# Four pairs of split weights, loads of summed blocks earlier in the program, and two dealing rates for the side pieces

## The chip, the core and the metric

The kernel runs on one core of one Trainium2 chip. The metric is device time in microseconds (us). PE is TensorE, the engine of the matmuls (PEld its weight loads), DVE is VectorE, ACT is ScalarE, POOL is GpSimd, and SP is the queue that issues nearly all loads.

## The reference

Three transformer-like layers on a batch of one, 256 tokens of 2048 channels, in float32: a layer with gated linear attention beside dilated attention, then a gated feed-forward of 5632 channels, then a retention and convolution layer, then a windowed attention layer. The part that matters here is the feed-forward:

```python
h2 = rms_norm(x, norm2_g[l])
x = x + (jax.nn.silu(h2 @ w_gate[l]) * (h2 @ w_up[l])) @ w_down[l]
```

`w_gate` and `w_up` are 2048 by 5632, `w_down` is 5632 by 2048. All weights are read once, 384 MB in float32.

## The kernel before

**Split products.** Each matrix product is made of three matmuls in a fast float32 form. Both operands are split into a high part (`hi`, rounded) and a low part (`lo`, what is left): `three` (line 184) issues xh·hi, xh·lo and xl·hi. A weight tile is 128 partitions by 2 by 512 (512 KB). `split` (line 158) makes one pair from it: a cast on ACT writes `hi` (line 160), a subtraction on DVE writes `lo` (line 161). The pairs live in the pool `hl_p`, which holds three of them: the cast of the fourth pair waits until PE has used the first.

**Streams.** `linear` (line 189) loads weight tiles into `raw` buffers (five of them), splits them, and multiplies each with both halves of the tokens: 12 matmuls of 512 columns for a tile. After each 3 matmuls it calls `deal` (line 178), which takes a piece from the deque `side` at every `pace[0]`-th call and writes it into the program at that point.

**The feed-forward stage.** The 5632 hidden channels are 11 blocks of 512. `plain(0)` computes block 0 directly. Then five passes follow (the loop over `w`, line 696): `seven(2w+1)` puts 28 side pieces into the deque; `plain(2w+2)` computes the next block as a stream (64 calls of `deal`); `down` multiplies two finished blocks with `w_down` (another 64 calls); `drain` empties what is left. The side pieces compute their block for gate and up with seven products instead of eight, in the manner of Strassen and Winograd: a product uses a half of the tokens alone, so a tile is worth 6 matmuls.

- Twelve pieces (`first`, line 634) load a tile into a `raw` buffer and split it, as a stream does.
- Sixteen pieces (`rest`, line 652; four steps `kp` of four pieces `n`) need sums of weight blocks. For each `kp` four blocks b12, b11, b22, b21 are loaded into a ring of six tiles (`block_tile`, line 610; the tags b0, b1, nh, nl, u10, u11, which show as `b` and `u` in a trace). Each piece then makes one DVE subtraction of 128 by 1024 (line 665, called a sum from here), splits its result and multiplies. The sums of a step are: n=0 needs b11 and b12, n=1 needs b12 and b22, n=2 needs b22 and b11, n=3 needs b22 and b21.

A tile of the ring is free for a new load once the last reader of its previous block is done: b22 of one step takes the tile of b12 of the step before, which the `lo` of that step's piece n=1 releases; b11 of one step takes the tile of b21 two steps before, and so on.

**What sets the order.** The program is written in the order just told, but a scheduler places the instructions of each engine by its own estimate of when their inputs are there. Each engine then runs its list in order: on DVE a sum that waits for a load holds up every `lo` behind it, and on SP a load that waits for its tile holds up every load behind it.

Of the kernel before, what the change touches and what calls it, by code (L numbers as in the profile page):

```python
# [25 lines left out]

CU, CR, CIND, CID, CMASK, COMASK, CGE, CLE, CGT, COROPE, CEND = 0, 128, 256, 258, 386, 514, 642, 770, 898, 1026, 1282


def _constants():  # L30
# [7 lines left out]
    c[:, CMASK:CMASK + P] = same & (s <= t)  # L38
    c[:, COMASK:COMASK + P] = np.where(s >= t, 0.0, NEG)
    c[:, CGE:CGE + P] = s >= t  # L40
    c[:, CLE:CLE + P] = s <= t
    c[:, CGT:CGT + P] = s > t

# [7 lines left out]
    co, so = angles(64)  # L51
    c[:, COROPE:COROPE + 128] = np.concatenate([co, co], 2).reshape(P, 128)
    c[:, COROPE + 128:COROPE + 256] = np.concatenate([-so, so], 2).reshape(P, 128)

# [24 lines left out]
def model(ctx, tc, a, out):  # L79
    nc = tc.nc  # L80
    cst = ctx.enter_context(tc.tile_pool(name="cst", bufs=1))
    raw_p = ctx.enter_context(tc.tile_pool(name="raw_p", bufs=5))
    hl_p = ctx.enter_context(tc.tile_pool(name="hl_p", bufs=3))
    xt_p = ctx.enter_context(tc.tile_pool(name="xt_p", bufs=4))
# [245 lines left out]
    for c0, n in ((2688, 400), (2304, 384), (2048, 256)):  # L330
        accs = linear(w_in, c0, n, full(st), got, fine=n == 400)
        got = []
        if n == 400:
            for b in range(4):
                got.append(fetch(w_in, b, 2304, 384))
                if b == 2:
                    tc.keep_in_program_order(nc.sync.dma_start(cm, a["c_main"]))
                cs = slice(b * 512, (b + 1) * 512)
# [7 lines left out]
            tc.keep_in_program_order(nc.gpsimd.dma_start(rb[0:32, :], a["rel_bias"]))  # L346
            sink = cst.tile([P, 32], F32, tag="sink", name="sink")
            tc.keep_in_program_order(nc.gpsimd.dma_start(sink, a["od_sinks_2"].partition_broadcast(P)))
            qkw = cst.tile([P, 2, 64], F32, tag="qkw", name="qkw")
            tc.keep_in_program_order(nc.gpsimd.dma_start(qkw[:, 0, :], a["od_q_norm_w_2"].partition_broadcast(P)))  # L350
            tc.keep_in_program_order(nc.gpsimd.dma_start(qkw[:, 1, :], a["od_k_norm_w_2"].partition_broadcast(P)))
            V.tensor_scalar(gc[:, NQ:NQ + 1], gc[:, NQ:NQ + 1], float(P) ** -0.5, None, ALU.mult)
# [277 lines left out]
    def seven(j):  # L630
# [4 lines left out]
        def first(kp, n):  # L635
# [14 lines left out]
            silu_gate(sg[:, 0], c11, rh[:, 0:1])  # L650

        def rest(kp, n):
            if n == 0:
                b12, b11, b22, b21 = [block_tile() for _ in range(4)]
                rows(b12, w_up, 2 * kp, c0)
                rows(b11, w_gate, 2 * kp, c0)
                rows(b22, w_up, 8 + 2 * kp, c0)
                rows(b21, w_gate, 8 + 2 * kp, c0)
                c["b"] = (b11, b12, b21, b22)
                if kp == 0:  # L660
                    c["P"] = [work_bank() for _ in range(3)] + [ps_acc.tile([P, 512], F32, tag="acc", name=nm("acc"))]
            b11, b12, b21, b22 = c["b"]
            dst, x0, x1, which = ((b11, b12, b11, "S1"), (b12, b22, b12, "S3"), (b22, b22, b11, "S2"),
# [6 lines left out]
        def last():  # L670
# [150 lines left out]

    ra = cst.tile([P, 2, 2, 64], F32, tag="ra", name="ra")
    rbt = cst.tile([P, 2, 2, 64], F32, tag="rbt", name="rbt")
    co = cm[:, COROPE:COROPE + 128].rearrange("p (t d) -> p t d", t=2)
    si = cm[:, COROPE + 128:COROPE + 256].rearrange("p (t d) -> p t d", t=2)
    for w in range(2):
# [52 lines left out]
    def att_scores(c):  # L879
# [47 lines left out]
    def att_turn(c):  # L927
# [5 lines left out]
        for k in range(t + 1):  # L933
# [117 lines left out]
```

## Time and profile before

| | us |
|---|---|
| median of 3 runs | 1947.53 (1945.02 to 1947.83) |
| the profiled execution, its own time | 1947.46 |
| its span on the core | 1945.7 |
| outside the span | 1.8 |

| engine | busy us | share of the span |
|---|---|---|
| PE | 1912.6 | 98% |
| DVE | 1280.0 | 66% |
| ACT | 970.4 | 50% |
| POOL | 193.3 | 10% |

The granted TensorE clock is full (1.00, the 2.4 GHz level) in every slice. PE's busy time is that of matmuls whose records overlap: each is recorded for some 390 ns, while the next starts 227 ns later, so a share of 98% does not say that matmuls start as often as they could. The feed-forward passes lie between about 500 and 1130 us of the span.

### The profile page before, as it was taken

The numbers are of one execution on the slowest core, as the hardware profiler recorded it, in microseconds if no ns is written. First come the engines' busy times: TensorE is split into PE (matmuls) and PEld (weight loads), VectorE is DVE, ScalarE is ACT, GpSimd is POOL, SyncE is SP. The second block draws the span as 40 slices with busy tenths as digits, with TensorE's granted clock in tenths as the row PEclk, the third lists the DMA queues.
The fourth block names the chain that finished last, engine by engine and source line by source line (L and its number), as shares of the span: only waits on it lengthen the run. The fifth ranks groups of instructions, "written<-read, shape, count | busy, mean of one in ns | idle before, by whom it ended". The sixth has DMA issues, their size and how long they took to land.

```text
span 1945.7 us, 23810 instructions
## 1 busy us (share of the span) xinstructions
PE 1912.6 (98%) x8808; PEld 1565.8 (80%) x8808; DVE 1280.0 (66%) x1486; ACT 970.4 (50%) x1313; POOL 193.3 (10%) x314
## 2 busy tenths in 40 slices
PE   8999999999999999999999999999999999999999
PEld 8877888888778778777777788888888888788787
DVE  5445555686787886886877875555555565777654
ACT  6544544455545545445445454444444454566543
POOL 2000221110000000000000001010000003754100
PEclk9999999999999999999999999999999999999999
DMA  8675665567778778777777566666666556544464
GB/s 303 196 213 150 179 174 173 172 203 250 239 218 248 229 224 256 230 228 239 244 226 244 191 175 183 174 182 172 186 193 192 188 183 191 166 138 133 141 200 146
DMA packets 202644, 387.72 MB, mean 199 GB/s; under 512 B 12296, under 2 KB 20512, under 8 KB 202400
## 3 DMA queue, kind: packets, MB, share of 16 engines
q1 hardware_dynamic: 201472, 382.52, 64.6%
q0 software_dynamic: 912, 3.64, 0.7%
q8 instruction: 69, 1.13, 0.2%
q14 instruction: 47, 0.39, 0.1%
q10 hardware_dynamic: 144, 0.05, 0.0%
HBM read 384.04 MB, written 3.68 MB: 199 GB/s over the span
## 4 chain that ended last, share of the span: by engine, by line
PE 82%; DVE 7%; DMA 6%; issue 3%; POOL 1%; ACT 1%; SPq 0%; DVEq 0%; ACTq 0%
PE acc L186 24%; PE acc L187 24%; PE acc L185 24%; DVE lo L161 4%; DMA raw<-in_w_down_dram 3%; DVE b L665 2%; DMA b<-in_w_up_dram 2%; PE at L187 2%; PE at L186 2%; PE at L185 2%; DVE u L665 1%; DMA u<-in_w_up_dram 1%; PE at L950 1%; ACT hi L160 1%; PE tr L223 1%
## 5 line engine op out<-in xcount | busy, mean ns | idle before, releaser
L161 DVE TENSOR_TENSOR lo<-raw,hi 128x1024 fp32r<-128x1024 f32 (+3 forms) x646 | 790.5, 1226 | 491.4 <-ACT hi L160 484.1
L160 ACT CAST hi<-raw 128x1024 fp32r<-128x1024 f32 (+3 forms) x646 | 670.8, 1039 | 696.6 <-PE acc L187 604.2
L186 PE MATMUL acc<-lo,xh 128*128 128x512 f32 (+3 forms) x1640 | 640.5, 391 | 3.4 <-DVE lo L161 3.4
L187 PE MATMUL acc<-hi,xl 128*128 128x512 f32 (+3 forms) x1640 | 634.6, 387 | 0.0
L185 PE MATMUL acc<-hi,xh 128*128 128x512 f32 (+3 forms) x1640 | 592.1, 389 | 5.3 <-ACT hi L160 5.3
L186 PEld LDWEIGHTS acc<-lo,xh 128*128 128x128 f32 x1640 | 308.9, 188 | 66.9 <-DVE lo L161 6.2
L185 PEld LDWEIGHTS acc<-hi,xh 128*128 128x128 f32 x1640 | 307.3, 188 | 68.5 <-ACT hi L160 5.6
L187 PEld LDWEIGHTS acc<-hi,xl 128*128 128x128 f32 x1640 | 309.0, 188 | 60.4 <-issue 2.1
L186 PE MATMUL acc<-lo,mh 128*128 128x512 f32 x640 | 253.9, 398 | 13.8 <-DVE lo L161 13.4
L187 PE MATMUL acc<-hi,ml 128*128 128x512 f32 x640 | 248.8, 391 | 0.0
L185 PE MATMUL acc<-hi,mh 128*128 128x512 f32 x640 | 231.7, 393 | 1.0 <-ACT mh L160 1.0
L186 PEld LDWEIGHTS acc<-lo,mh 128*128 128x128 f32 x640 | 120.1, 188 | 49.9 <-DVE lo L161 26.3
L185 PEld LDWEIGHTS acc<-hi,mh 128*128 128x128 f32 x640 | 119.4, 188 | 26.3 <-ACT mh L160 1.2
L187 PEld LDWEIGHTS acc<-hi,ml 128*128 128x128 f32 x640 | 120.1, 188 | 23.9 <-DVE ml L161 0.2
L160 ACT CAST hi<-b 128x1024 fp32r<-128x1024 f32 x54 | 57.0, 1055 | 90.5 <-PE acc L187 90.5
L161 DVE TENSOR_TENSOR lo<-b,hi 128x1024 fp32r<-128x1024 f32 x54 | 65.8, 1219 | 20.6 <-ACT hi L160 20.6
L709 POOL DMA_DIRECT2D u<-in_c_even_dram x1 | 0.6, 635 | 679.5 <-PE at L187 679.5
L186 PE MATMUL at<-lo,u 128*128 128x512 f32 x160 | 62.9, 393 | 4.1 <-DVE lo L161 4.1
L187 PE MATMUL at<-hi,u 128*128 128x512 f32 x160 | 62.4, 390 | 0.0
L185 PE MATMUL at<-hi,u 128*128 128x512 f32 x160 | 62.3, 389 | 0.0
L252 DVE TENSOR_TENSOR x<-x,acc 128x512 f32<-128x512 f32 x88 | 57.2, 679 | 6.9 <-PE acc L187 6.9
L665 DVE TENSOR_TENSOR b<-b,b 128x1024 f32<-128x1024 f32 x41 | 50.0, 1219 | 11.8 <-DMA b<-in_w_up_dram 11.2
(252 smaller groups left out, 1554.9 us busy)
## 6 DMA issues: line engine op xcount, KB each, us to landing
raw<-in_ev_w_in_dram SPq DMA_DIRECT2D x128, 512.0 KB, 3.8
raw<-in_w_gate_dram SPq DMA_DIRECT2D x88, 512.0 KB, 4.4
raw<-in_w_down_dram SPq DMA_DIRECT2D x88, 512.0 KB, 4.8
raw<-in_w_in_dram SPq DMA_DIRECT2D x80, 512.0 KB, 3.8
raw<-in_od_w_in_dram SPq DMA_DIRECT2D x72, 512.0 KB, 3.6
raw<-in_w_up_dram SPq DMA_DIRECT2D x68, 512.0 KB, 4.6
raw<-in_w_out_dram SPq DMA_DIRECT2D x32, 512.0 KB, 3.6
raw<-in_ev_w_out_dram SPq DMA_DIRECT2D x32, 512.0 KB, 3.7
```

The costliest lines, as they stand in the source:

```text
L160: A.copy(hi, src)
L161: V.tensor_tensor(lo, src, hi.bitcast(F32), ALU.subtract)
L185: T.matmul(o, xh, hi, start=start, stop=False)
L186: T.matmul(o, xh, lo, start=False, stop=False)
L187: T.matmul(o, xl, hi, start=False, stop=stop)
L223: T.transpose(ps[:, k * S + t * P:k * S + (t + 1) * P], x[:, t, c:c + P], ident)
L252: V.tensor_tensor(xs, xs, accs[t], ALU.add)
L665: V.tensor_tensor(dst, x0, x1, ALU.subtract)
L709: nc.gpsimd.dma_start(ce, a["c_even"][:, :512])
L950: T.matmul(pv[e * 64:(e + 1) * 64, :S], vo[:, k, g * 64:(g + 1) * 64], PT[:, :, e], start=k == 0, stop=k == t)
```

## The change

Three edits concern the feed-forward stage:

1. `hl_p` holds four pairs of split weights, not three.
2. The loads of the summed blocks are taken out of `rest` and written by a new function `ahead`, which is called four pieces earlier: those of step 0 in the last four of the twelve first pieces, those of step kp+1 in the pieces of step kp.
3. The pieces are dealt at two rates: the twelve without a sum at every 1.75 calls on average, the sixteen with a sum at every 5.75 calls (before: all at every 4). `deal` keeps the fraction that is left over.

The fourth pair takes 8 KB a partition. The room comes from moving and sharing small tiles: the constants of the last layer (masks, rotation tables, the q and k norm weights, the sinks) are no longer loaded at the start into tiles of their own, but after the feed-forward, by POOL, into the ring's tiles `b0` and `b1`; the scratch tile `junk` is now one of the three `junk2`.

```diff
-    hl_p = ctx.enter_context(tc.tile_pool(name="hl_p", bufs=3))
+    hl_p = ctx.enter_context(tc.tile_pool(name="hl_p", bufs=4))
...
-    cm = cst.tile([P, CEND], F32, tag="cm", name="cm")
+    cm = cst.tile([P, CODD], F32, tag="cm", name="cm")
...
             if pace[1] >= pace[0]:
-                pace[1] = 0
+                pace[1] -= pace[0]
                 side.popleft()()
...
-            junk = sm.tile([P, 512], F32, tag="junk", name=nm("junk"), bufs=1)
+            junk = sm.tile([P, 512], F32, tag="junk2", name=nm("junk"), bufs=3)
...
             times(c[n], ("A11", "S4", "A12")[n], parts(raw), kp)
+            if n == 2:
+                ahead(0, kp)
...
+        def ahead(kp, n):
+
+            if kp > 3:
+                return
+            for i in ((0, 1), (), (2,), (3,))[n]:
+                b = c["b", kp, i] = block_tile()
+                rows(b, (w_up, w_gate, w_up, w_gate)[i], (0, 0, 8, 8)[i] + 2 * kp, c0)
+
         def rest(kp, n):
+            ahead(kp + 1, n)
             if n == 0:
-                b12, b11, b22, b21 = [block_tile() for _ in range(4)]
-                rows(b12, w_up, 2 * kp, c0)
-                rows(b11, w_gate, 2 * kp, c0)
-                rows(b22, w_up, 8 + 2 * kp, c0)
-                rows(b21, w_gate, 8 + 2 * kp, c0)
-                c["b"] = (b11, b12, b21, b22)
                 if kp == 0:
+                    pace[0] = 5.75
...
+        pace[0] = 1.75
         side.extend([lambda kp=kp, n=n: first(kp, n) for kp in range(4) for n in range(2)])
...
         seven(2 * w + 1)
-        pace[0] = 4
         plain(2 * w + 2)
...
+    co_ = raw_p.tile([P, 960], F32, tag="b0", name="co_", bufs=1)
+    nc.gpsimd.dma_start(co_[:, :CEND - CODD], a["c_main"][:, CODD:])
...
+    tabs = raw_p.tile([P, 2, 2, 2, 64], F32, tag="b1", name="tabs", bufs=1)
```

**Place 1: DVE, first pass, around the sum that needs b22 of step 1.** `lo` rows whose source is `raw` belong to streams and first pieces, those with `b` or `u` as source to summed blocks; rows of line 665 (668 after) are sums. The load of b22 (`b_4349` before, `b_4157` after) takes the tile that the `lo` from `b_4199` (after: `b_3982`) releases. Before:

```order
L161 TENSOR_TENSOR lo_4213<-b_4200,hi_4212 128x1024
L649 TENSOR_TENSOR c_4175<-c_4014,at_4073 128x512
L161 TENSOR_TENSOR lo_4223<-raw_4180,hi_4222 128x1024
L296 SCALAR_TENSOR_TENSOR u_847_4174<-u_847_4174,c_4175 128x512
L161 TENSOR_TENSOR lo_4240<-b_4199,hi_4239 128x1024
L161 TENSOR_TENSOR lo_4254<-raw_4249,hi_4253 128x1024
L665 TENSOR_TENSOR u_887_4347<-b_4349,u_887_4347 128x1024
L161 TENSOR_TENSOR lo_4271<-b_4201,hi_4270 128x1024
L665 TENSOR_TENSOR b_4349<-b_4349,u_888_4348 128x1024
L161 TENSOR_TENSOR lo_4281<-raw_4250,hi_4280 128x1024
L665 TENSOR_TENSOR b_4350<-b_4349,b_4350 128x1024
L161 TENSOR_TENSOR lo_4298<-b_4202,hi_4297 128x1024
```

After:

```order
L163 TENSOR_TENSOR lo_4115<-b_3982,hi_4114 128x1024
L163 TENSOR_TENSOR lo_4145<-raw_4140,hi_4144 128x1024
L298 SCALAR_TENSOR_TENSOR u_830_4053<-u_830_4053,c_4054 128x512
L163 TENSOR_TENSOR lo_4161<-b_4030,hi_4160 128x1024
L668 TENSOR_TENSOR u_832_4064<-b_4157,u_832_4064 128x1024
L298 SCALAR_TENSOR_TENSOR u_848_4133<-u_848_4133,acc_3793 128x512
L668 TENSOR_TENSOR b_4157<-b_4157,u_833_4066 128x1024
L298 SCALAR_TENSOR_TENSOR u_848_4133<-u_848_4133,acc_3794 128x512
L163 TENSOR_TENSOR lo_4174<-raw_4141,hi_4173 128x1024
L668 TENSOR_TENSOR b_4189<-b_4157,b_4189 128x1024
L163 TENSOR_TENSOR lo_4193<-b_4051,hi_4192 128x1024
L163 TENSOR_TENSOR lo_4207<-raw_4202,hi_4206 128x1024
```

Between the releasing `lo` and the sum stood one `lo`; now two stand there and a shorter operation. The sum still stands directly behind.

**Place 2: DVE, towards the end of a pass, around the sum that needs b11 of the next pass's step 0.** (`x` rows add finished `w_down` products.) That b11 (`u_1068_5215` before, `u_1026_4999` after) takes the tile that the `lo` from `u_916_4478` (after: `u_890_4346`) releases. Before:

```order
L161 TENSOR_TENSOR lo_4526<-raw_4521,hi_4525 128x1024
L161 TENSOR_TENSOR lo_4543<-u_915_4477,hi_4542 128x1024
L665 TENSOR_TENSOR b_4603<-b_4605,b_4603 128x1024
L161 TENSOR_TENSOR lo_4553<-raw_4522,hi_4552 128x1024
L665 TENSOR_TENSOR b_4605<-b_4605,b_4604 128x1024
L161 TENSOR_TENSOR lo_4570<-u_916_4478,hi_4569 128x1024
L665 TENSOR_TENSOR b_4606<-b_4605,b_4606 128x1024
L161 TENSOR_TENSOR lo_4588<-raw_4583,hi_4587 128x1024
L252 TENSOR_TENSOR x<-x,acc_4453 128x512
L252 TENSOR_TENSOR x<-x,acc_4454 128x512
L161 TENSOR_TENSOR lo_4613<-b_4604,hi_4612 128x1024
L665 TENSOR_TENSOR u_1068_5215<-u_1067_5214,u_1068_5215 128x1024
```

After:

```order
L668 TENSOR_TENSOR b_4409<-b_4495,b_4409 128x1024
L163 TENSOR_TENSOR lo_4499<-u_885_4314,hi_4498 128x1024
L163 TENSOR_TENSOR ml_4365<-tr_4373,mh_4364 128x512
L668 TENSOR_TENSOR b_4495<-b_4495,b_4411 128x1024
L163 TENSOR_TENSOR lo_4518<-raw_4485,hi_4517 128x1024
L668 TENSOR_TENSOR b_4527<-b_4495,b_4527 128x1024
L254 TENSOR_TENSOR x<-x,acc_4380 128x512
L163 TENSOR_TENSOR lo_4531<-u_890_4346,hi_4530 128x1024
L254 TENSOR_TENSOR x<-x,acc_4381 128x512
L163 TENSOR_TENSOR lo_4551<-raw_4546,hi_4550 128x1024
L668 TENSOR_TENSOR u_1026_4999<-u_1025_4997,u_1026_4999 128x1024
L163 TENSOR_TENSOR lo_4568<-b_4411,hi_4567 128x1024
```

Between the releasing `lo` and that sum stood a sum, two `lo` and two adds; now an add and one `lo`.

**Place 3: SP, first pass, where the loads of step 1 stand among the stream's.** Rows with `raw` are loads of the stream, the others those of summed blocks. Before:

```order
L124 DMA raw_4327<-in_w_down_dram 128x2x512
L124 DMA raw_4328<-in_w_down_dram 128x2x512
L124 DMA b_4350<-in_w_gate_dram 128x2x512
L124 DMA raw_4393<-in_w_down_dram 128x2x512
L124 DMA b_4349<-in_w_up_dram 128x2x512
L124 DMA raw_4394<-in_w_down_dram 128x2x512
L124 DMA b_4475<-in_w_up_dram 128x2x512
L124 DMA raw_4455<-in_w_down_dram 128x2x512
```

After:

```order
L126 DMA raw_4202<-in_w_up_dram 128x2x512
L126 DMA b_4189<-in_w_gate_dram 128x2x512
L126 DMA raw_4203<-in_w_up_dram 128x2x512
L126 DMA raw_4253<-in_w_up_dram 128x2x512
L126 DMA b_4157<-in_w_up_dram 128x2x512
L126 DMA raw_4254<-in_w_up_dram 128x2x512
L126 DMA b_4232<-in_w_up_dram 128x2x512
L126 DMA raw_4300<-in_w_up_dram 128x2x512
```

They stood between loads of `w_down`; now they stand among those of `w_up`, that is, in the stream of the second product of `plain`.

## Rows read from the trace of the kernel before

**Rows 1.** Page: PE's line of busy us, share of the span and instructions.

```profile
PE 1912.6 (98%) x8808; PEld 1565.8 (80%) x8808; DVE 1280.0 (66%) x1486; ACT 970.4 (50%) x1313; POOL 193.3 (10%) x314
```

**Rows 2.** Windows: length, busy us (instructions) by engine, granted clock, DMA share, GB/s.

```profile
400.00:500.00 100.00, 100.00 (x455) 82.97 (x454) 75.92 (x79) 56.50 (x66) 5.14 (x5) 1.00 0.75 232
500.00:1100.00 600.00, 579.09 (x2537) 465.64 (x2536) 474.56 (x462) 305.69 (x311) 0.78 (x2) 1.00 0.74 233
```

**Rows 3.** Waits of PE, 500 to 1130 us: us in total, times, longest.

```profile
PE acc L186 <- DVE lo L161: 16.4, 23, 1.2
PE at L186 <- DVE lo L161: 4.1, 5, 1.0
```

**Rows 4.** Waits of DVE, 500 to 1130 us.

```profile
DVE lo L161 <- ACT hi L160: 91.0, 90, 3.1
DVE u L665 <- DMA b<-in_w_up_dram: 14.1, 6, 3.6
DVE b L665 <- DMA b<-in_w_up_dram: 11.2, 6, 3.4
DVE b L665 <- DMA u<-in_w_up_dram: 11.0, 6, 3.6
```

**Rows 5.** Timeline, all engines, first pass: start, us, instruction, idle before.

```profile
505.30 0.39 PE L187 MATMUL acc<-hi,xl 128*128 128x512 f32 x1
...
506.87 1.23 DVE L161 TENSOR_TENSOR lo<-b,hi 128x1024 fp32r<-128x1024 f32 x1 [0.58 <-ACT hi L160]
...
508.12 0.37 SPq L124 DMA_DIRECT2D b<-in_w_up_dram  x1
508.22 1.23 DVE L161 TENSOR_TENSOR lo<-raw,hi 128x1024 fp32r<-128x1024 f32 x1
...
509.15 0.39 PE L186 MATMUL acc<-lo,xh 128*128 128x512 f32 x1
...
513.04 1.23 DVE L665 TENSOR_TENSOR u<-b,u 128x1024 f32<-128x1024 f32 x1 [3.60 <-DMA b<-in_w_up_dram]
...
514.19 1.22 DVE L161 TENSOR_TENSOR lo<-b,hi 128x1024 fp32r<-128x1024 f32 x1
515.32 1.22 DVE L665 TENSOR_TENSOR b<-b,u 128x1024 f32<-128x1024 f32 x1
...
515.46 0.50 PE L186 MATMUL at<-lo,u 128*128 128x512 f32 x1 [0.93 <-DVE lo L161]
...
517.73 0.50 PE L186 MATMUL acc<-lo,xh 128*128 128x512 f32 x1 [0.60 <-DVE lo L161]
```

**Rows 6.** Timeline of DVE, fifth pass, the same sum.

```profile
1050.16 1.22 DVE L665 TENSOR_TENSOR b<-u,b 128x1024 f32<-128x1024 f32 x1 [3.62 <-DMA u<-in_w_up_dram]
```

**Rows 7.** Timeline of PE around six transposes of a finished block.

```profile
729.46 0.82 PE L548 MATMUL tr<-cm,u 128*128 128x128 f32 x6
...
730.58 0.39 PE L186 MATMUL at<-lo,u 128*128 128x512 f32 x1
```

**Rows 8.** Groups of instructions, 500 to 1130 us: count, busy us, mean ns, idle before.

```profile
L160 ACT CAST hi<-raw 128x1024 fp32r<-128x1024 f32 x199 | 209.6, 1053 | 170.0 <-PE acc L187 114.4 <-PE at L187 47.8 <-issue 5.3
L161 DVE TENSOR_TENSOR lo<-raw,hi 128x1024 fp32r<-128x1024 f32 x200 | 243.7, 1220 | 63.1 <-ACT hi L160 59.2
L252 DVE TENSOR_TENSOR x<-x,acc 128x512 f32<-128x512 f32 x40 | 25.9, 678 | 0.0
```

**Rows 9.** Loads: landing of `raw` (500 to 1100 us), a start load, a start window.

```profile
DMA to landing us min/median/max: 3.5/4.6/6.5
raw<-in_w_in_dram SPq DMA_DIRECT2D x6, 400.0 KB, 7.8
20.00:25.00 5.00, 5.00 (x30) 5.00 (x29) 3.37 (x4) 2.42 (x3) 0.00 (x0) 1.00 1.06 402
```

**Rows 10.** POOL's load at the stage's end; PE's only wait behind 1130 us.

```profile
1099.09 0.64 POOL L709 DMA_DIRECT2D u<-in_c_even_dram  x1 [679.49 <-PE at L187]
PE tr L931 <- POOL Lx L925: 1.3, 1, 1.3
```

More of the change, by code (lines that the diff above doesn't have):

```diff
@@ L24 @@
 NEG = -1e30
-CU, CR, CIND, CID, CMASK, COMASK, CGE, CLE, CGT, COROPE, CEND = 0, 128, 256, 258, 386, 514, 642, 770, 898, 1026, 1282
+CU, CR, CIND, CID, CMASK, CODD, CEND = 0, 128, 256, 258, 386, 514, 1282
+COMASK, CGE, CLE, CGT, COROPE, CQK, CSINK, CNSINK = 0, 128, 256, 384, 512, 768, 896, 928
 def _constants():
@@ L38, in _constants @@
     c[:, CMASK:CMASK + P] = same & (s <= t)
[L39 to L42, printed above, removed]
+    c[:, CODD + COMASK:CODD + COMASK + P] = np.where(s >= t, 0.0, NEG)
+    c[:, CODD + CGE:CODD + CGE + P] = s >= t
+    c[:, CODD + CLE:CODD + CLE + P] = s <= t
+    c[:, CODD + CGT:CODD + CGT + P] = s > t
     def angles(d):
@@ L51, in _constants @@
     co, so = angles(64)
-    c[:, COROPE:COROPE + 128] = np.concatenate([co, co], 2).reshape(P, 128)
-    c[:, COROPE + 128:COROPE + 256] = np.concatenate([-so, so], 2).reshape(P, 128)
+    c[:, CODD + COROPE:CODD + COROPE + 128] = np.concatenate([co, co], 2).reshape(P, 128)
+    c[:, CODD + COROPE + 128:CODD + COROPE + 256] = np.concatenate([-so, so], 2).reshape(P, 128)
     ce, se = angles(256)
@@ L271, in finish_head @@
         for t in range(2):
-            junk = sm.tile([P, 512], F32, tag="junk", name=nm("junk"), bufs=1)
+            junk = sm.tile([P, 512], F32, tag="junk2", name=nm("junk"), bufs=3)
             A.activation(junk[:, :S], po[:, t * S:(t + 1) * S], AF.Square, accum_out=s[:, t:t + 1])
@@ L346, in model @@
             tc.keep_in_program_order(nc.gpsimd.dma_start(rb[0:32, :], a["rel_bias"]))
[L347 to L351, printed above, removed]
             V.tensor_scalar(gc[:, NQ:NQ + 1], gc[:, NQ:NQ + 1], float(P) ** -0.5, None, ALU.mult)
@@ L650, in first @@
             silu_gate(sg[:, 0], c11, rh[:, 0:1])
+        def ahead(kp, n):
[4 more added lines that the diff above has]
+                rows(b, (w_up, w_gate, w_up, w_gate)[i], (0, 0, 8, 8)[i] + 2 * kp, c0)
         def rest(kp, n):
+            ahead(kp + 1, n)
             if n == 0:
-                b12, b11, b22, b21 = [block_tile() for _ in range(4)]
-                rows(b12, w_up, 2 * kp, c0)
-                rows(b11, w_gate, 2 * kp, c0)
-                rows(b22, w_up, 8 + 2 * kp, c0)
-                rows(b21, w_gate, 8 + 2 * kp, c0)
-                c["b"] = (b11, b12, b21, b22)
                 if kp == 0:
+                    pace[0] = 5.75
                     c["P"] = [work_bank() for _ in range(3)] + [ps_acc.tile([P, 512], F32, tag="acc", name=nm("acc"))]
-            b11, b12, b21, b22 = c["b"]
+            b12, b11, b22, b21 = [c["b", kp, i] for i in range(4)]
             dst, x0, x1, which = ((b11, b12, b11, "S1"), (b12, b22, b12, "S3"), (b22, b22, b11, "S2"),
@@ L707, in model @@
     ev_w_in, ev_w_out = a["ev_w_in_2"][0], a["ev_w_out_2"][0]
+    co_ = raw_p.tile([P, 960], F32, tag="b0", name="co_", bufs=1)
+    nc.gpsimd.dma_start(co_[:, :CEND - CODD], a["c_main"][:, CODD:])
+    nc.gpsimd.dma_start(co_[:, CQK:CQK + 64], a["od_q_norm_w_2"].partition_broadcast(P))
+    nc.gpsimd.dma_start(co_[:, CQK + 64:CQK + 128], a["od_k_norm_w_2"].partition_broadcast(P))
+    nc.gpsimd.dma_start(co_[:, CSINK:CSINK + 32], a["od_sinks_2"].partition_broadcast(P))
+    qkw = co_[:, CQK:CQK + 128].rearrange("p (w d) -> p w d", w=2)
+    sink, nsink = co_[:, CSINK:CSINK + 32], co_[:, CNSINK:CNSINK + 32]
     ce, gam_all = unit(9, [512]), unit(10, [4, S])
@@ L820, in model @@
     mixT = mix_pairs()
[L822 to L825, printed above, removed]
+    tabs = raw_p.tile([P, 2, 2, 2, 64], F32, tag="b1", name="tabs", bufs=1)
+    ra, rbt = tabs[:, 0], tabs[:, 1]
+    co = co_[:, COROPE:COROPE + 128].rearrange("p (t d) -> p t d", t=2)
+    si = co_[:, COROPE + 128:COROPE + 256].rearrange("p (t d) -> p t d", t=2)
     for w in range(2):
@@ L871, in model @@
     oT = []
-    omask = cm[:, COMASK:COMASK + P]
-    nsink = small([32], "nsink")
+    omask = co_[:, COMASK:COMASK + P]
     G.tensor_scalar(nsink, sink, -1.0, None, ALU.mult)
@@ L909, in att_scores @@
             A.copy(L, pls[0])
-            V.copy_predicated(L4, four(cm[:, CGE:CGE + P]).bitcast(I32), pls[1].rearrange("p (h k) -> p h k", h=4))
+            V.copy_predicated(L4, four(co_[:, CGE:CGE + P]).bitcast(I32), pls[1].rearrange("p (h k) -> p h k", h=4))
             V.tensor_reduce(mx[:, hs], L4, AX.X, ALU.max)
```

4 lines of the change are left out of this document (2 added, 2 removed).

## Prediction

> **What bounds the kernel now.** I read the page first, then the busy times by stretch, then the waits of PE and of the engine that it names, then one pass as a timeline. PE is busy for 98% of the span [rows 1] at the full granted clock of 1.00 (2.4 GHz) [rows 2], so the span can only shrink where PE waits or starts matmuls late. Between 500 and 1100 us it is busy for 579.09 of 600 us, ahead of that for 100 of 100 [rows 2]. Behind 1130 us it waits once, for 1.3 us [rows 10]. So the five feed-forward passes are the place.
>
> What is lost there is more than the idle time, since matmul records overlap. Matmuls follow each other every 0.2265 us: 17 of them between 505.30 and 509.15 [rows 5]. A pass has 128 calls of `deal` with 3 matmuls each and 28 pieces with 6, so 552 matmuls, 125.0 us, and 16 transposes, each 0.11 us: six of them and two matmuls take 1.12 us in [rows 7]. That makes 126.8 us. The same late sum stands at 513.04 in the first pass and at 1050.16 in the fifth [rows 5, 6]: 134.28 us a pass. **7.5 us a pass are lost**, 33.5 us in the 600 (4.47 passes). The count agrees: 2537 matmuls [rows 2], 71 of them transposes, need 566 us. 33.5 us is the most that this stage can give.
>
> By idle time alone, 600 less 579.09, it would be 21 us [rows 2]. The Trainium skill (Perfetto Trace Analysis, Identifying the Most-Contended Engine) says that matmul busy time misjudges PE's headroom and the weight loads' busy share is the one to judge by: 465.64 us at the 0.8297 of the undisturbed stretch need 561 us, so 39 would be lost [rows 2]. The period lies between, nearer to the rule.
>
> Why PE waits: it waits for `lo` from DVE, 28 times [rows 3]. DVE isn't short of time on the whole (474.56 of 600 us busy), but its sums wait for loads, 36.3 us in 18 waits [rows 4]. In [rows 5] a `lo` ends at 508.1, the load of b22 is issued at 508.12 and the sum starts at 513.04, 4.9 us later. DVE does nothing for 3.60 us, and every `lo` behind the sum is late. From one `lo` (508.22) to the end of the next (514.19 to 515.32) pass 7.1 us, less 1.135 of the first: 5.97. PE then waits 0.93, and 0.60 once more before it has caught up.
>
> **A reserve.** On DVE one operation of 1024 columns follows the last after 1.135 us (514.19 to 515.32 [rows 5]); one of 512 takes 0.62 by the mean of 678 ns less the same overlap [rows 8]. The cast of a pair starts when PE has used the pair 3 (after: 4) before it, and its `lo` is ready 1.05 + 1.22 = 2.27 us later [rows 8]. A stream's pair is worth 12 matmuls or 2.72 us, a piece's 6 or 1.36. With one of each in turn, PE has in hand at best 3 x 2.04 - 2.27 = 3.85 us when a `lo` is done. The 5.97 us above are 2.1 more; the two stalls show 1.53 idle and about 0.17 hidden by the record's length in each, 1.9. The picture holds.
>
> **Part 1, the fourth pair.** In the new mix (1.44 stream pairs for each sum piece) the mean pair is 2.16 us, and four are worth 4 x 2.16 - 2.27 = 6.4 us in hand. It costs no instruction. Casts may run earlier, and so `raw` tiles come free earlier.
>
> **Part 2, the loads.** In the order the sums that were late still follow closely on the `lo` that frees the tile, because the ring still has six tiles and the scheduler already put loads and sums as early as they can go. At place 1 the work between rises from one `lo` (1.135) to 2.9 us; at place 2 it falls from 4.6 to 1.75 us. Taking 4.9 us from that `lo` to the sum, the new order leaves seven waits in a pass, of 0.8, 1.5, 1.9, 2.6, 2.0, 3.1 and 1.4 us: 13.3 us, where the trace has 36.3/5 = 7.3. So this part by itself makes DVE wait more, not less. There is room: 0.79 x 134.28 = 106.2 us of work and 13.3 of waits are 119.5 in a pass of 126.8. Bounds of the part alone, in DVE's time: from -7.3 (all waits gone) to +14.4 us a pass (the longest, 3.1, seven times, less 7.3). I take +6, as the order has it.
>
> **Part 3, the dealing.** A call of `deal` is 0.68 us of PE. Before, a sum piece stands every 4 calls: PE has 4.08 us, DVE a stream `lo`, a sum, its `lo` and a share of the adds to x (8 in 64 calls), 3.7 us, to which 0.46 of waits come: more than PE's time, so nothing is ever refilled. At 5.75 calls PE has 5.27 us, DVE 1.44 x 1.135 + 2.27 + 0.45 = 4.35, and 0.83 of waits: 5.18. That is just enough. The twelve other pieces (1.75 calls) have 2.55 us of PE and 1.6 of DVE, so each pass begins with the full reserve. 12 x 1.75 + 16 x 5.75 = 113 calls of 128, as 112 before: nothing is pushed into `drain`.
>
> **The sum.** I followed one pass through the new DVE order with these prices, adding 2.72 or 1.36 for each pair and taking off what DVE does and waits for up to the next `lo`. From 5.9 us at place 1 the balance falls to 0.4 and 0.9, climbs to 5.6, falls to 1.9, climbs to 7.2, and then has low points of 1.0, 1.0, 0.8 and 0.4. At place 2 the sum for the next pass's b11 asks for 1.135 x 2 and a wait of 3.1, 5.4 us, with 3.1 in hand: **2.3 us short**. That place exists in four of the five passes: 9.2 us stay. Landings spread from 3.5 to 6.5 us around 4.6 [rows 9], so I let one in four of the low points of 1 us and less, some five in each of five passes, cost 0.5: 3 us. The gain is 33.5 - 9.2 - 3 = 21.3 us. From the profiled execution's own 1947.46 (span 1945.7 and 1.8 around it; the median of three is 1947.53) that is 1926.2, say **1926 us**.
>
> **What costs nothing.** The shorter constants at the start leave PE's first matmuls as they are; their loads come later in SP's order. POOL loads the rest after the passes, behind its load at 1099.09 [rows 10], and works out sink and rotation tables before the statistics of the next layer, 13 short operations behind a landing that I bound by 7.8 us, the slowest in [rows 9]: done before the last `down` ends near 1130. If that cover failed it would cost under 10 us once. PE's one wait behind 1130 us is 1.3 us and may come or go.
>
> **Rivals.**
>
> A. *The late sums keep PE waiting.* The balance runs near zero from place 1 on. If a load takes 5.5 us to its sum rather than 4.9, seven waits grow by 0.6, 4.2 us a pass. The margins hold about 1 of it, so 2.3 + 3.2 = 5.5 us a pass stay, 27 in all: a gain of 6 us, 1941. For: more waits in the new order; largest landing 6.5 [rows 9]. Against: in the sum stretch loads come at (1 + 1.44) x 0.524 MB in 5.27 us, 243 GB/s, hardly more than the 233 now [rows 2].
>
> B. *The first pieces outrun the loads (slower).* At 1.75 calls they want 1.44 tiles in 2.55 us, 295 GB/s. Five `raw` tiles then turn over in 8.9 us, of which cast and `lo` take 2.3. Up to a landing of 6.5 us, the longest now, nothing is lost. At 7.8, as at the start [rows 9], 0.25 us on each of 17 tiles, 4.2 a pass, is within the 7 us in hand. From about 10 us it eats the gain (0.69 x 17 - 7 = 4.6 a pass, 23 in all); at 11.5 it is 49 us less 21: 1975. Against: the start moved 402 GB/s [rows 9].
>
> C. *The fourth pair brings no reserve*, since PE starts a new pair before it is through with older ones and holds their buffers. In hand are then 3 x 2.16 - 2.27 = 4.2 us, 2.2 less at every low point: five of them fall 1.2 to 1.8 short, 7.5 us a pass in all, as now: 1947. For: at place 2 the new PE order mixes two streams' tiles. Against: elsewhere it uses pairs in the order in which DVE makes them. This is also the case in which the change does not do what its words say, as part 2 already hardly does.
>
> **How the numbers follow.** Forecast 0.70, A 0.17, C 0.07, B 0.06. The range reaches from nearly all of the 33.5 us gained (1914) to A (1942). It leaves out B, C and a part of A. A measurement of this kernel can tell about 0.2% (3.9 us) from no change. Faster by more: the forecast and most of A (0.13), 0.83; within: the rest of A and C, 0.11; slower: B, 0.06.
>
> **What would show it.** The pass shrinks from 134.3 to about 129.5 us. PE's waits for `lo` (20.5 us now) fall to some 8, and what is left stands at the sum for the next pass's b11. DVE's waits for loads do not fall: 36 us now, more after, up to 66. If they vanish, part 2 is wrong; if PE still waits for `lo` in three or more places of a pass, the reserve is; if PE or ACT wait for `raw` loads among the first pieces, B has happened.

## The result, and the profile after

| | median us | runs | range |
|---|---|---|---|
| before | 1947.68 | 4 | 1945.02 to 1948.1 |
| after | 1927.87 | 4 | 1926.19 to 1928.69 |

The ratio is 0.9900, 95% interval 0.9883 to 0.9917: 19.8 us or 1.0% faster. The forecast was 1926 us. The span of the profiled executions went from 1945.7 to 1924.4 us.

The page of after, PE's line; [rows 1] answer to it.

```profile
PE 1906.0 (99%) x8808; PEld 1567.0 (81%) x8808; DVE 1276.6 (66%) x1486; ACT 968.9 (50%) x1313; POOL 201.1 (10%) x315
```

Busy time by stretch, after (length, busy us and instructions by engine, granted clock, DMA share, GB/s); before: [rows 2].

```profile
400.00:500.00 100.00, 100.00 (x454) 82.64 (x452) 79.21 (x84) 57.90 (x68) 5.14 (x5) 1.00 0.75 237
500.00:1100.00 600.00, 594.23 (x2634) 485.31 (x2634) 487.23 (x479) 313.03 (x320) 9.25 (x19) 1.00 0.74 240
```

Read the count of matmuls, not the busy time: 2537 before, 2634 now. With the prediction's prices (0.2265 us a matmul, 0.11 a transpose, 71 of these) 2634 are worth 588.3 us. 11.7 of the 600 us are still lost, where it was 33.7. (The traces have 72 to 80 transposes in this stretch; with their true number the loss is 0.1 to 1.0 us larger, most in the fastest kernels.) The gain lies in the feed-forward passes, as forecast.

Waits of PE, after, 500 to 1130 us (us in total, times, longest); before: [rows 3].

```profile
PE tr L545 <- DVE u L556: 5.3, 4, 1.9
...
PE at L188 <- DVE lo L163: 0.3, 1, 0.3
```

Waits of DVE in the same stretch; before: [rows 4].

```profile
DVE lo L163 <- ACT hi L162: 51.3, 62, 3.1
DVE b L668 <- DMA u<-in_w_up_dram: 13.6, 6, 3.1
DVE b L668 <- DMA b<-in_w_gate_dram: 13.2, 5, 3.3
DVE u L668 <- DMA b<-in_w_up_dram: 11.0, 6, 2.5
DVE b L668 <- DMA b<-in_w_up_dram: 10.6, 6, 2.5
DVE u L668 <- DMA u<-in_w_gate_dram: 6.5, 3, 3.1
```

PE's waits for `lo` fell from 20.5 us to 0.3. DVE's waits for loads did not fall: 54.9 us in 26 waits, where [rows 4] have 36.3; three more waits of sums, 5.2 us, have no releaser in the profile. So the sums are later than before, and PE doesn't notice. What PE notices is new: it waits for line 556, where `plain` multiplies `up` into the finished block ahead of its transposes (line 545).

DVE's timeline, after, at that place in the first and the fifth pass (start, us, instruction, idle before):

```profile
528.53 1.23 DVE L668 TENSOR_TENSOR b<-b,b 128x1024 f32<-128x1024 f32 x1 [3.29 <-DMA b<-in_w_gate_dram]
529.67 1.40 DVE L556 SCALAR_TENSOR_TENSOR u<-acc,r2h,u 128x512 f32<-128x512 f32 x2
...
1046.19 1.40 DVE L556 SCALAR_TENSOR_TENSOR u<-acc,r2h,u 128x512 f32<-128x512 f32 x2
```

PE's timeline beside the first of them:

```profile
527.23 0.39 PE L189 MATMUL acc<-hi,ml 128*128 128x512 f32 x1
...
528.14 0.39 PE L187 MATMUL at<-hi,u 128*128 128x512 f32 x1
530.48 0.33 PE L545 MATMUL tr<-cm,u 128*128 128x128 f32 x1 [1.95 <-DVE u L556]
```

The sum for b11 of step 3 stands 3.29 us before its load, the two operations of line 556 stand behind the sum, and PE's transposes stand behind them. From 529.67 to 1046.19 four passes go by: 129.1 us a pass, where it was 134.28 [rows 5, 6] and some 129.5 were forecast.

By the starts of PE's matmuls 6.0 of the 11.7 us stand at the transposes of four passes and 1.1 at four late `lo`; the rest is spread over starts that are 0.15 us late or less.

### The profile page after: what moved, and what is told of

Its sections match the earlier page's. It is cut to its first block, busy times and chain, and to the rows that moved or that the text cites. A ratio compares the mean times of both kernels' runs of the same rounds, so it can differ in the third digit from the quotient of the medians.

```text
span 1924.4 us, 23805 instructions
## 1 busy us (share of the span) xinstructions
PE 1906.0 (99%) x8808; PEld 1567.0 (81%) x8808; DVE 1276.6 (66%) x1486; ACT 968.9 (50%) x1313; POOL 201.1 (10%) x315
## 4 chain that ended last, share of the span: by engine, by line
PE 89%; DMA 4%; DVE 4%; issue 1%; POOL 1%; ACT 0%; SPq 0%; DVEq 0%; ACTq 0%
PE acc L188 25%; PE acc L187 25%; PE acc L189 25%; PE at L188 2%; PE at L189 2%; PE at L187 2%; DVE lo L163 2%; DMA b<-in_w_up_dram 2%; DMA b<-in_w_gate_dram 1%; PE at L960 1%; DVE b L668 1%; DMA u<-in_w_up_dram 1%; PE tr L225 1%; PE tr L307 1%; DMA u<-in_w_gate_dram 0%
## 5 line engine op out<-in xcount | busy, mean ns | idle before, releaser
L187 PE MATMUL acc<-hi,xh 128*128 128x512 f32 (+3 forms) x1640 | 622.7, 390 | 5.7 <-ACT hi L162 5.7
L187 PE MATMUL acc<-hi,mh 128*128 128x512 f32 x640 | 247.1, 393 | 1.0 <-ACT mh L162 1.0
```

The lines of the kernel that those rows point to most:

```text
L187: T.matmul(o, xh, hi, start=start, stop=False)
```

## The experiments

Twelve kernels. "Lost" is 600 us less what the matmuls between 500 and 1100 us are worth, counted as above. "Load waits" are DVE's waits for loads, 500 to 1130 us. Ratios are to the kernel before, run beside each. Its own median beside them was 1947.7 us for after, 1948.0 for no_early_loads and the three `only_` kernels, 1945.6 for the `pinned_` ones, 1945.4 for the next three and 1946.0 for the last; so medians of different groups differ by some 2 us that are not the kernels', and the ratios decide there.

| kernel | pairs | dealing | place of the sums | median us | ratio (95%) | lost us | load waits us |
|---|---|---|---|---|---|---|---|
| before | 3 | 4 | scheduler's | 1947.7 | 1 | 33.7 | 36.7 (with 0.4 in a group that [rows 4] leave out) |
| only_moved_tiles | 3 | 4 | scheduler's | 1949.7 | 1.0006 (0.9997 to 1.0015) | 33.9 | 36.1 |
| only_four_pairs | 4 | 4 | scheduler's | 1936.6 | 0.9943 (0.9930 to 0.9955) | 23.0 | 45.6 |
| only_dealing | 3 | 1.75/5.75 | scheduler's | 1970.8 | 1.0116 (1.0102 to 1.0130) | 54.0 | 69.7 |
| after | 4 | 1.75/5.75 | scheduler's | 1927.9 | 0.9900 (0.9883 to 0.9917) | 11.7 | 54.9 |
| no_early_loads | 4 | 1.75/5.75 | scheduler's | 1928.9 | 0.9901 (0.9887 to 0.9915) | 14.2 | 59.0 |
| pinned_sums | 4 | 1.75/5.75 | at their own piece | 1953.8 | 1.0045 (1.0033 to 1.0058) | 32.1 | 0 |
| pinned_three_pairs | 3 | 1.75/5.75 | at their own piece | 1961.3 | 1.0085 (1.0071 to 1.0098) | 38.4 | 0 |
| pinned_three_pairs_old_dealing | 3 | 4 | at their own piece | 1977.8 | 1.0170 (1.0156 to 1.0184) | 56.8 | 0 |
| pinned_four_pairs_old_dealing | 4 | 4 | at their own piece | 1977.5 | 1.0167 (1.0153 to 1.0181) | 55.4 | 0 |
| ring_of_eight_three_pairs | 3 | 1.75/5.75 | scheduler's | 1966.1 | 1.0108 (1.0095 to 1.0122) | 47.9 | 71.7 |
| sums_one_piece_ahead | 4 | 1.75/5.75 | a piece ahead | 1914.9 | 0.9845 (0.9832 to 0.9859) | 1.5 | 0 |
| sums_ahead_three_pairs_old_dealing | 3 | 4 | a piece ahead | 1915.1 | 0.9847 (0.9834 to 0.9860) | 1.7 | 0 |
| before_with_sums_ahead | 3 | 4 | a piece ahead | 1914.2 | 0.9842 (0.9829 to 0.9856) | 1.5 | 0 |

### Each part alone

Theory: the fourth pair is a reserve and brings the gain, the dealing helps to refill it, the loads written ahead do nothing. Rival: the loads or the dealing carry the gain. First, after with the second edit undone:

```diff
-            if n == 2:
-                ahead(0, kp)
...
-            ahead(kp + 1, n)
             if n == 0:
+                for m in range(4):
+                    ahead(kp, m)
                 if kp == 0:
```

> The changed kernel with the loads of summed blocks written in the piece that needs them, as before; four pairs and the two dealing rates stay. The order of every engine's instructions comes out as in the changed kernel, row for row when buffer numbers are left out. Theory (the scheduler had already put these loads as early as their tiles allow): no difference from the changed kernel, 1928 us, and DVE's sums wait for loads as long as there, some 58 us. Rival (earlier loads carry part of the gain): slower than the changed kernel by 5 us or more, 1933 to 1945.

1928.9 us: no difference. The lists of instructions of the two kernels are the same on all engines; only the numbers of the buffers differ. So here a load goes where its tile comes free, wherever the program writes it.

The other three have this edit undone too. only_four_pairs besides deals as before:

```diff
-                    pace[0] = 5.75
+                    pace[0] = 4
...
-        pace[0] = 1.75
+        pace[0] = 4
```

> Of the three edits of the feed-forward only the fourth pair (with the moved constants that make room for it); every piece dealt at 4 calls, loads as before. Theory (a reserve in front of DVE's late sums): the running balance of the prediction, made for this order, is short by 22 us over the five passes where it is short by 34 before, so a gain of 12 us, 1936. Rival 1 (the fourth pair alone carries the gain): 1928. Rival 2 (the dealing alone carries it): 1947.

1936.6 us, 11 less than before: the size that the theory gave it. Its waits of PE between 500 and 1130 us, beside [rows 3]:

```profile
PE acc L188 <- DVE lo L163: 14.1, 13, 2.2
```

only_dealing keeps the new dealing and has three pairs:

```diff
-    hl_p = ctx.enter_context(tc.tile_pool(name="hl_p", bufs=4))
+    hl_p = ctx.enter_context(tc.tile_pool(name="hl_p", bufs=3))
```

> Of the three edits only the dealing: twelve pieces at 1.75 calls, sixteen at 5.75, with three pairs and loads as before. Theory (a reserve in front of late sums): the new order has longer waits for loads on DVE (67 us by the balance, 37 in the order before) and three pairs don't cover them; the balance is short by 46 us where it is short by 34 before, so slower than before by up to 12 us, 1947 to 1960. Rival (DVE's time in the sum stretch is what PE waited for, and thinner dealing gives it): faster, 1930 to 1938.

1970.8 us, 23 more than before: that it helps by itself has fallen, and the harm is larger than the theory allowed. DVE's waits for loads, 500 to 1130 us:

```profile
DVE b L667 <- DMA b<-in_w_up_dram: 16.0, 6, 3.3
DVE b L667 <- DMA u<-in_w_up_dram: 15.5, 6, 3.7
DVE u L667 <- DMA b<-in_w_up_dram: 15.4, 6, 3.0
DVE b L667 <- DMA b<-in_w_gate_dram: 14.1, 12, 1.9
DVE u L667 <- DMA u<-in_w_gate_dram: 8.7, 6, 1.9
```

They are nearly twice those of [rows 4], with the loads written where they always were. So it is the dealing that makes the sums later, not the edit on the loads. With three pairs nothing takes that up: PE waits for `lo` 41 times. With four pairs the same dealing is worth 8.7 us (1936.6 to 1927.9), and with the new dealing the fourth pair is worth 43 us, alone 11. The two parts can't be priced one by one.

only_moved_tiles has both of these edits, so that the moved constants are all that is left of the change:

> None of the three edits of the feed-forward, only what makes room for the fourth pair: the last layer's constants loaded behind the feed-forward into the ring's tiles, and the shared scratch tile. Theory: as before, 1947.5 us within 2. Rival (moving the constants out of the start, or out of POOL's way, gives or costs something): over 4 us either way.

1949.7 us, beside 1948.0 of before: the same. The constants that POOL loads behind the passes cost nothing that can be told.

### The sums at their own piece

What is left in after are sums that stand before loads. The scheduler puts a sum close behind the `lo` that frees the load's tile, as if the load took less than the 4.9 us that [rows 5] show. One edit keeps the sums where the program writes them:

```diff
-            V.tensor_tensor(dst, x0, x1, ALU.subtract)
+            tc.keep_in_program_order(V.tensor_tensor(dst, x0, x1, ALU.subtract))
```

> After, with one edit: the sums of weight blocks keep their place in the program, at their own piece, instead of being placed just behind the `lo` that frees the load's tile. Between that `lo` and the sum then lie at least 13.7 us of DVE work, worked out from the order with the prediction's durations, where a load takes 4.9 us to its sum. In the changed kernel DVE waits for loads some 57 us in the five passes, and PE loses about 12 us between 500 and 1100 us, before the transposes of a finished block and at few other places. Theory (what is left of the stalls is DVE standing before loads): DVE's waits for loads fall below 5 us, PE's wait for the operation of line 556 goes, and the time is 1914 to 1921 us, 7 to 12 less than 1928. Rival 1 (a sum made at its piece comes too late for the piece's own `hi` and `lo`, and PE waits for these): 1928 or more, with PE's waits for `lo` above 10 us. Rival 2 (the rest of the loss is not DVE's loads but the adds and transposes themselves): 1926 to 1929.

1953.8 us: a miss of over 30 us. DVE does not wait for a load once between 500 and 1130 us, and the wait for line 556 is gone, as the theory has it. But the loss moved. PE's largest wait in that stretch:

```profile
PE at L187 <- ACT hi L162: 18.2, 4, 4.5
```

PE's timeline around one of these waits:

```profile
622.02 0.39 PE L189 MATMUL at<-hi,xl 128*128 128x512 f32 x1
626.96 0.50 PE L187 MATMUL at<-hi,u 128*128 128x512 f32 x1 [4.55 <-ACT hi L162]
```

And ACT's at the same place:

```profile
623.17 0.72 ACT L297 ACTIVATE u<-c,st_rh 128x512 f32<-128x512 f32 x1 [6.47 <-DVE c L648]
625.86 1.04 ACT L162 CAST hi<-u 128x1024 fp32r<-128x1024 f32 x1 [1.97 <-DVE u L668]
```

Step 0's first sum now stands behind the end of the last first piece: PE must finish that piece's product, DVE adds it (line 648), ACT takes the tanh (line 297), DVE multiplies, and only then come the sum and its cast. For all that time PE has nothing to do. There is one such stall in each pass (the first at 491 us, ahead of the stretch that "lost" counts), and behind each the granted clock falls (0.98 on the mean of the stretch; the last section shows such a fall):

```profile
500.00:1100.00 600.00, 580.60 (x2544) 475.45 (x2543) 470.62 (x458) 293.55 (x311) 0.00 (x0) 0.98 0.71 232
```

The three others add to this edit the ones on the pairs (`bufs=3`), on the dealing (`pace[0] = 4` in both places), or both, as shown above.

> As pinned_sums, but three pairs of split weights (the new dealing stays). Without the fourth pair and without the pinned sums the new dealing gave 1970.8. Theory (the fourth pair is a reserve against DVE's waits for loads, and against little else): with no such waits three pairs are nearly enough, 1916 to 1924, at most 4 us above pinned_sums. Rival (four pairs are needed in any case, for DVE's chains of two sums and two `lo`, or for the adds): 1935 or more, with PE's waits for `lo` above 10 us.

1961.3 us: it has the same stalls. Set against pinned_sums the fourth pair is worth 7 us, more than the 4 that the theory allowed, and far less than the 43 that it is worth where sums wait for loads.

> Three pairs, all pieces dealt at every 4 calls as in the kernel before, sums pinned: against the kernel before the loads written ahead and the pinned sums are all that is left (beside the moved small tiles). Theory: DVE has 3.7 us of work for 4.08 us of PE in the sum stretch and no waits, so the balance stays within the reserve of 3.85 us save for some 1 us a pass where adds and sums meet: 1918 to 1928. Rival (the dealing is what counts, since DVE at 91% cannot refill the reserve): 1938 or more.

> Four pairs, every 4 calls, sums pinned. Theory: as pinned_sums, 1914 to 1921. If the new dealing is worth something of its own: 4 us or more above pinned_sums.

1977.8 and 1977.5 us: the theories missed by 50 us and more, and the rivals' bounds are passed: here the new dealing is worth 24 us (1977.5 to 1953.8). The fourth pair makes no difference at all. DVE's timeline of the kernel with four pairs shows why:

```profile
510.30 1.22 DVE L668 TENSOR_TENSOR b<-b,b 128x1024 f32<-128x1024 f32 x1
512.71 1.23 DVE L163 TENSOR_TENSOR lo<-b,hi 128x1024 fp32r<-128x1024 f32 x1 [1.20 <-ACT hi L162]
513.86 1.22 DVE L163 TENSOR_TENSOR lo<-raw,hi 128x1024 fp32r<-128x1024 f32 x1
514.99 1.22 DVE L668 TENSOR_TENSOR b<-b,b 128x1024 f32<-128x1024 f32 x1
```

A sum stands right ahead of its own cast and `lo`, so DVE stands 1.20 us for the cast. A piece then takes 3.7 + 1.2 = 4.9 us of DVE, where every 4 calls give 4.08 of PE: 0.82 short at 16 pieces, 13.1 a pass, 59 in the 4.47 passes between 500 and 1100 us. 56.8 and 55.4 are lost. A reserve bridges a delay; it does nothing where an engine is short of time at every piece. At 5.75 calls the piece has 5.27 us of PE. By an estimate with the prediction's prices DVE then needs 4.35 + 1.2 = 5.55 us, 4.5 a pass too much, which is within the 6.4 us that four pairs hold; in pinned_sums PE does not wait for a `lo` once between 500 and 1130 us.

### The sums a piece ahead

So a sum should stand late enough for its load and early enough for its cast. Each piece now writes the sum of the next one, behind its own split; the first sum stands ahead of the last first piece.

```diff
+            if n == 2 and kp == 3:
+                ahead(0, 3)
+                sums(0, 0)
             times(c[n], ("A11", "S4", "A12")[n], parts(raw), kp)
...
+        def sums(kp, n):
+            b12, b11, b22, b21 = [c["b", kp, i] for i in range(4)]
+            dst, x0, x1 = ((b11, b12, b11), (b12, b22, b12), (b22, b22, b11), (b21, b22, b21))[n]
+            tc.keep_in_program_order(V.tensor_tensor(dst, x0, x1, ALU.subtract))
+            c["s", kp, n] = dst
...
+            times(c["P"][n], ("S1", "S3", "S2", "A22")[n], parts(c["s", kp, n]), kp)
+            if 4 * kp + n < 15:
+                sums(kp + n // 3, (n + 1) % 4)
```

> After, with each sum pinned one piece earlier than its own (the first one ahead of the last piece without a sum, the others behind the split of the piece before), so that it stands neither behind the add and tanh of the last first piece nor right ahead of its own cast. pinned_sums (1953.8) lost nothing at the old places; it lost five stalls of 4.5 us, where the cast of step 0 stood on ACT behind that tanh, and a fall of the granted clock behind each of them; its DVE also stood 1.2 us before each `lo` of a sum. In the new order the load leads the sum by at least 13 us of DVE work and a `lo` of the stream lies between sum and own `lo`. Theory (what bounds the changed kernel is nothing but the place of the sums on DVE): no wait of PE above 1 us in the passes, DVE's load waits under 3 us, 1911 to 1917 us, near the 1914 at which all of the 33.5 us are gained. Rival (casts and `lo` of the summed blocks, or the adds, keep a loss of their own): 1922 or more.

> The same order of sums, with three pairs and every piece at every 4 calls, as in the kernel before: neither the fourth pair nor the new dealing is in it. Theory (both are only a reserve against sums that wait for loads): within 5 us of sums_one_piece_ahead, 1912 to 1921. Rival (DVE at 3.7 us of 4.08 refills too slowly behind the adds, and a reserve of 3.85 us is too small even without waits for loads): 1930 or more.

1914.9 and 1915.1 us: both hits. They take 1.5% less than before, after 1.0%, so they are 10 to 11 us faster than after (13 by the medians, 2 of which before shows too). Neither the fourth pair nor the dealing is needed.

The last kernel takes the kernel before, with all three edits left out, and moves its sums in the same way; the four loads of a step are written with its first sum:

```diff
+        def sums(kp, n):
+            if n == 0:
+                loads(kp)
+            b11, b12, b21, b22 = c["b"]
...
-            V.tensor_tensor(dst, x0, x1, ALU.subtract)
-            times(c["P"][n], which, parts(dst), kp)
+            times(c["P"][n], ("S1", "S3", "S2", "A22")[n], parts(c["s", kp, n]), kp)
+            if 4 * kp + n < 15:
+                sums(kp + n // 3, (n + 1) % 4)
```

> The kernel before (three pairs, every piece at every 4 calls, small tiles where they were) with one edit: each sum pinned one piece ahead of its own, and the four loads of a step written with its first sum, one piece ahead and not four. Theory (the place of the sums on DVE is the whole of the loss, and where loads stand in the program is nothing, since the scheduler moves them to where their tile comes free): as sums_ahead_three_pairs_old_dealing, 1915 us, 1913 to 1918. Rival (with loads written a single piece ahead they are issued late and DVE waits for them again): DVE's load waits above 20 us and 1922 or more.

1914.2 us (1914.0 to 1914.27), 1.6% faster than before. It beats both kernels of this case; from the two above it does not differ clear of noise (ratios 0.9842, 0.9845 and 0.9847). Its passes in the view of busy time by stretch:

```profile
500.00:1100.00 600.00, 599.03 (x2679) 494.94 (x2679) 505.45 (x495) 320.10 (x328) 1.18 (x2) 1.00 0.74 243
```

DVE's timeline around a sum (line 667):

```profile
510.89 1.22 DVE L161 TENSOR_TENSOR lo<-b,hi 128x1024 fp32r<-128x1024 f32 x1 [0.20 <-ACT hi L160]
512.04 1.22 DVE L667 TENSOR_TENSOR b<-b,b 128x1024 f32<-128x1024 f32 x1
513.17 1.22 DVE L161 TENSOR_TENSOR lo<-raw,hi 128x1024 fp32r<-128x1024 f32 x1
514.97 1.23 DVE L161 TENSOR_TENSOR lo<-b,hi 128x1024 fp32r<-128x1024 f32 x1 [0.58 <-ACT hi L160]
```

A stream's `lo` stands between a sum and its own `lo`, which hides the cast. 2679 matmuls are worth 598.5 us (597.5 with the trace's 80 transposes).

### Tiles in place of the fourth pair

Two more tiles for the ring take the 8 KB that the fourth pair took:

```diff
-    hl_p = ctx.enter_context(tc.tile_pool(name="hl_p", bufs=4))
+    hl_p = ctx.enter_context(tc.tile_pool(name="hl_p", bufs=3))
...
-        i = ring[0] % 6
+        i = ring[0] % 8
...
+        if i > 5:
+            return raw_p.tile([P, 2, 512], F32, tag=f"b{i - 4}", name=nm("b"), bufs=1)
```

> After, with the 8 KB a partition spent on two more tiles in the ring of summed blocks (eight) in place of the fourth pair; new dealing, sums where the scheduler puts them. A tile comes free two blocks earlier, so the order has no wait for a load at 4.9 us, and a hand-followed balance that falls short by only 0.8 us in four places. Theory (only the waits for loads matter, it is the same whether tiles or order remove them): DVE's load waits under 10 us, 1914 to 1924, against 1970.8 with six tiles. Rival (the sums, placed still earlier by the scheduler, crowd the `lo` of the streams, or three pairs are too few): 1935 or more.

1966.1 us: a miss. DVE's waits for loads, 500 to 1130 us, are as many as in only_dealing:

```profile
DVE b L670 <- DMA b<-in_w_up_dram: 34.9, 18, 2.7
DVE u L670 <- DMA b<-in_w_up_dram: 20.9, 9, 3.6
DVE u L670 <- DMA u<-in_w_up_dram: 15.6, 8, 4.0
```

The expectation was wrong in its reading of the order: it looked for the `lo` that frees a tile six blocks back, where it is eight. Read rightly, the work between that `lo` and the sum is between 1.1 and 2.4 us at most sums that need an `up` block. The scheduler uses the earlier tile to put the sum earlier, close behind the load again. An example from the first pass, DVE's rows with the issue of the load (SPq) between them; one `lo` stands between the `lo` that ends at 524.23 and the sum:

```profile
523.01 1.22 DVE L163 TENSOR_TENSOR lo<-b,hi 128x1024 fp32r<-128x1024 f32 x1
524.15 1.22 DVE L163 TENSOR_TENSOR lo<-raw,hi 128x1024 fp32r<-128x1024 f32 x1
524.26 0.37 SPq L126 DMA_DIRECT2D b<-in_w_up_dram  x1
528.79 1.23 DVE L670 TENSOR_TENSOR u<-b,u 128x1024 f32<-128x1024 f32 x1 [3.42 <-DMA b<-in_w_up_dram]
```

More room gives no slack where the order eats it.

## Why the prediction was right, and where it was not

**The place and the price of the stage: right.** The most that the passes could give was worked out as 33.5 us. The last kernel got 33.2 by the spans of the profiled executions (1945.7 to 1912.5) and 31.9 by the medians run side by side (1946.0 to 1914.2). By the weight loads' busy share the prediction had 39 us lost; here the period of the matmuls was the better ruler, and the busy time (21 us) the worse one. The prediction left out half of what it drew on there: that section of the Trainium skill (Perfetto Trace Analysis, Identifying the Most-Contended Engine) names MFU, the arithmetic done as a share of the peak's, beside the weight loads' busy share. To count matmuls is to measure in that way.

**Part 1, the fourth pair: right in its mechanism.** Alone it gives 11 us, with the dealing PE's waits for `lo` all but vanish. Rival C, that it is no reserve, has fallen. The figure of 6.4 us in hand was not measured by itself.

**Part 2, the loads: the wait was right, its cause wrong.** DVE's waits rose to 54.9 us, within the 66 that were named. But the prediction booked them on the loads edit ("this part by itself makes DVE wait more"). That edit changes no list at all; the waits come with the dealing (69.7 us in only_dealing) and a little with the pairs (45.6). The step that failed was to compare the orders of before and after, with all edits in, and to read the difference as the work of one.

**Part 3, the dealing: right only beside the fourth pair.** "Just enough" described the balance with 6.4 us in hand. With three pairs the prediction had 4.2 in hand and low points 1.2 to 1.8 us short, and from that 1947 us (rival C's arithmetic). That case was run, as only_dealing: 1970.8. The mechanism shows, but 54.0 us are lost, not 33.5. Two things were not in the arithmetic: more waits for loads (69.7 us, where 13.3 a pass make some 60 in this stretch), and stalls at the transposes (4.4 us in four waits) with a fall of the clock behind them. How much of the missing 20 us each is worth was not separated.

**The sum: right in size, wrong in place.** Left over were to be 9.2 us at the sum for the next pass's b11, four times 2.3, and 3 us elsewhere: 12.2. Counted are 11.7. But PE waits for a `lo` once, 0.3 us, where some 8 were forecast, and 5.3 us go to the transposes of `plain`, in four waits. The step that failed followed pairs alone through DVE. The two operations of line 556 use no pair, so no reserve stands between them and PE: PE stands as far as the sum ahead of them ends later than their input is ready. In the first pass the product that the first of them reads has its last matmul at 527.23, the sum starts at 528.53 and line 556 at 529.67. By an estimate from these starts some 0.8 of PE's 1.95 us are the wait for the load and 1.14 the sum itself.

The term for the next pass's b11 came to nothing: DVE stands at that sum 2.13, 2.17, 2.13 and 2.01 us in the four passes, where 3.1 was taken, and PE does not wait behind it. The first of the four:

```profile
551.94 1.23 DVE L668 TENSOR_TENSOR u<-u,u 128x1024 f32<-128x1024 f32 x1 [2.13 <-DMA u<-in_w_gate_dram]
```

That is 1 of the 2.3 us that were to be short. Where the rest went was not separated; while PE stands at the transposes it uses up no pairs, which may refill the reserve. That the two terms are of one size is chance.

**Rivals A and B: not seen.** Late sums do keep PE waiting, as A has it, but at the transposes and not for `lo`, and the time is 1927.9, not 1941. As to B, loads did not hold up the first pieces; ACT waits for `raw` loads in after, 500 to 1130 us:

```profile
ACT hi L162 <- DMA raw<-in_w_up_dram: 3.8, 6, 1.0
```

**What the prediction did not ask:** why the sums stood where they stood. It saw that the scheduler puts them right behind the load and took that as given. All three edits work around that place; moving the sums does away with the loss, and then they are worth nothing. The Trainium skill (Perfetto Trace Analysis, Optimization Strategy) says that a gap which keeps coming back can mean that there are too few buffers. The gap here came back in every pass, and a fourth pair did help by 11 us; but two more ring tiles brought next to nothing (1.0108 of before, beside 1.0116 of only_dealing with six), and with the old number of buffers and another order it is gone (1914.2). The measurement decides for the order.

## What to carry to other kernels

Where an in-order engine waits for a load, look first at where the waiting instruction stands in its list: one piece earlier or later may do more than another buffer. Here the scheduler spent two more tiles on putting the sums earlier, as if a load were shorter than it is. A fixed place has two bounds: behind the load's landing, and ahead of its own consumers by more than the steps between them on other engines, with nothing of another chain in front of it. And price a reserve together with what draws on it: parts that each lose or gain alone (23 us more, 11 less) can give 20 us less together.

## What the runs showed of the hardware

The granted TensorE clock fell behind stalls of 1.2 to 2 us. PE in only_dealing, where it stood for 1.20 us at the transposes and 1.23 us at the next `lo`:

```profile
579.96 0.39 PE L187 MATMUL acc<-hi,mh 128*128 128x512 f32 x1
581.55 0.41 PE L545 MATMUL tr<-cm,u 128*128 128x128 f32 x2 [1.20 <-DVE u L684]
583.19 0.74 PE L188 MATMUL acc<-lo,mh 128*128 128x512 f32 x1 [1.23 <-DVE lo L163]
583.73 0.63 PE L189 MATMUL acc<-hi,ml 128*128 128x512 f32 x1
584.15 0.63 PE L188 MATMUL acc<-lo,mh 128*128 128x512 f32 x1
584.58 0.63 PE L189 MATMUL acc<-hi,ml 128*128 128x512 f32 x1
```

The granted clock of that stretch:

```profile
583.00:588.00 5.00, 4.81 (x14) 3.86 (x15) 4.36 (x6) 0.64 (x1) 0.00 (x0) 0.66 0.72 226
```

Part of it ran at the lower of the two levels (1.2 GHz): matmuls follow each other every 0.43 us, not every 0.2265, for eight of them, so 1.6 us come on top of the 2.4 us of idle time. It happens at this place in four passes. The same stall need not bring it: in after 1.95 us at the transposes left the clock at 1.00 over the next 5 us; in no_early_loads, whose lists are the same, 1.94 us brought it down to 0.66.

The stretch behind the stall in after:

```profile
531.00:536.00 5.00, 5.00 (x25) 4.11 (x24) 4.87 (x6) 3.46 (x4) 0.00 (x0) 1.00 0.47 147
```

And in no_early_loads, behind its stall at 918.49:

```profile
919.00:924.00 5.00, 5.00 (x18) 3.94 (x17) 3.58 (x4) 1.84 (x2) 0.00 (x0) 0.66 0.51 154
```

PE has 25 instructions in one, 18 in the other. So a stall of some 2 us can cost nearly twice its length (7 starts of 0.2265 us, 1.6 us more), and does not each time.
